# MLP down projections in seven quadrant products, their sums carried through PSUM by ScalarE, with a feature-major output

## The chip, the core and the metric

The kernel runs on one core of one Trainium2 chip. A core has TensorE (PE) for matrix products, which reads SBUF and writes PSUM; VectorE (DVE) and ScalarE (ACT) for element-wise work on both memories; GpSimd (POOL), which is little used here; and SyncE (SP), which issues nearly all DMA loads. Each engine runs its own instructions in order and waits on semaphores for the others. The metric is device time of one execution in microseconds (us), the median of three runs.

## What is computed

A trunk of two layers over 512 tokens with 1024 features: a latent-attention mixer (MLA), then a gated linear attention mixer (GLA). Each is followed by a squared-ReLU MLP with 4096 hidden features. Only the MLP and the last norm change.

```python
def sq_relu_mlp(xn, w_up, w_down):
    hid = jnp.square(jax.nn.relu(xn @ w_up))
    return hid @ w_down
...
for i in range(DEPTH):                       # 2: MLA, GLA
    x = x + mixer(rms_norm(x, norm_mix[i]))
    x = x + sq_relu_mlp(rms_norm(x, norm_mlp[i]), w_up[i], w_down[i])
return rms_norm(x, final_norm)
```

## The kernel before

**Layout.** The residual stream lies in SBUF feature-major: `xT[j]` holds features 128j to 128j+127 on the partitions and 512 tokens along the free dimension. A weight tile of 128 by 128 is the stationary operand, and up to 512 tokens stream past it. All products are made in float32 accuracy from two rounded halves: a value is split into `hi` (a rounding ScalarE copy, line 76) and `lo` (a VectorE subtraction, line 79), and `mm3` (lines 81 to 86) issues three matmuls, hi by hi, hi by lo, lo by hi. A `piece` (line 109) is such a split of 1024 weight values per partition, in three rotating buffers `wh` and `wl`. So every piece costs one ScalarE and one VectorE instruction, and a piece feeds 24 matmuls.

**Order.** The kernel is written as straight-line Python. A planner puts each engine's instructions in order: by the order of the source where it can, and otherwise an instruction that is ready earlier goes first. Tiles with the same tag share a fixed number of buffers; an instruction that needs a buffer waits until its last reader is done. SP's loads wait in the same way, one behind the other.

**Up projection.** 4096 hidden features are handled in 8 blocks of 512 (`FB`). The first block, `up(0)` (line 715), is a plain product: 96 matmuls of 512 tokens. Blocks 1 to 7 are made by `up_fast` (line 825) in seven products of quadrants instead of eight, after Strassen and Winograd: the weights are halved by input features and by output features, the activations by features and by tokens (`first`, `second`: tokens 0 to 255 and 256 to 511). The sums of activation quadrants, T1 to T4, are made once per layer by `quadrants` (line 806); the sums of weight quadrants are VectorE instructions on 1024 values per partition, once per block (lines 855, 856, 864, 865). Each product has 24 matmuls of 256 tokens. Its result is added to others by VectorE (`add`, line 840); `finish` (line 843) applies ReLU, the norm's factor `nrm.rstd` and the square, and splits the result for the down projection.

**Down projection.** `down` (line 736) is a plain product: for each block of 512 hidden features 8 output tiles of 12 matmuls over 512 tokens. VectorE adds each result from PSUM into `xT` (line 750). For the last block of the last layer `down_final` (line 756) makes tokens 0 to 255 feature-major and tokens 256 to 511 row-major, so that most of the last norm runs while PE still works. The class `Final` (line 1311) does that norm and writes two outputs.

**Around it.** `out_proj` (line 690) makes the mixers' output projection in four steps of two feature tiles, adds them to `xT` and calls `nxt.add`, which scales, splits and squares a tile for the next norm. `Norm.finish` (line 216) makes the mean with a matmul (line 218) and `rsqrt` with two ScalarE and three VectorE instructions. After the first MLP comes `gla` (line 895), whose first products use the norm's tiles in order. PSUM has eight banks of 512 float32 per partition, in three tags (`bank`, line 62).

Of the kernel before, what the change touches and what calls it, by code (L numbers as in the profile page):

```python
# [25 lines left out]
TH = S // 2  # L26
MH = 8
# [21 lines left out]
def trunk_kernel(ctx: ExitStack, tc: tile.TileContext, t_in: dict, out: bass.AP, out_row: bass.AP):  # L49
# [5 lines left out]
    ps = ctx.enter_context(tc.tile_pool(name="ps", bufs=1, space=bass.MemoryType.PSUM))  # L55
    count = [0]

# [4 lines left out]
    def bank(tag):  # L62
        return ps.tile([P, 512], F32, tag=f"ps_{tag}", bufs={"a": 2, "b": 3, "c": 3}[tag], name=uname("ps"))

    def tmp(shape=(P, 512), dt=F32):
        return sb.tile(list(shape), dt, tag="tmp", bufs=6, name=uname("tmp"))

    def slot(tag, shape=(P, 512)):
        return sb.tile(list(shape), F32R, tag=f"set_{tag}", bufs={"A": 16, "B": 16}[tag], name=uname("set"))
# [11 lines left out]
    def mm3(psum, w, x, start, stop):  # L81
        wh, wl = w
        xh, xl = x
        PE.matmul(psum, wh, xh, start=start, stop=False)  # L84
        PE.matmul(psum, wh, xl, start=False, stop=False)  # L85
        PE.matmul(psum, wl, xh, start=False, stop=stop)  # L86
# [17 lines left out]
    def load(src, a, n):  # L104
        raw = sb.tile([P, a, n], F32, tag="wraw", bufs=2, name=uname("wraw"))
        SP.dma_start(raw, src)
        return raw
# [78 lines left out]
    class Norm:  # L186
# [7 lines left out]
        def square(self, src):  # L194
            if self.seen == 0:
                self.acc = sb.tile([P, S], F32, tag="acc", bufs=2, name=uname("acc"))
# [19 lines left out]
        def finish(self):  # L216
            m = bank("c")
            PE.matmul(m, self.inv, self.acc, start=True, stop=True)  # L218
            r = sb.tile([P, S], F32, tag="rstd", bufs=2, name=uname("rstd"))
            rsqrt(r, m, S)  # L220
            self.rstd = r
            return r

# [103 lines left out]
    def mla(layer, nrm, first, pools):  # L327
# [70 lines left out]
        rows = sb.tile([3 * RB, S], F32, tag="rstd", bufs=2, name=uname("rstd"))  # L398
# [3 lines left out]
        raw = sb.tile([P, 2, MH, VD], F32, tag="wraw", bufs=2, name="wraw_v")  # L402
# [12 lines left out]
        for t in range(NT):  # L415
# [18 lines left out]
            if t == 1:  # L434
                wide = bank("c")
                PE.matmul(wide, ones128[0:1], rows[0:1], start=True, stop=True)
                r_kv = sb.tile([P, S], F32, tag="rstd", bufs=2, name=uname("rstd"))
# [21 lines left out]
        raw = sb.tile([P, 3, MH, ROPE], F32, tag="wraw", bufs=2, name="wraw_qr")  # L459
# [18 lines left out]
        def project(h, tag="a"):  # L478
            if h % 4 == 0:
                raw = sb.tile([P, 3, 4, NOPE], F32, tag="wraw", bufs=2, name=uname("wraw_qn"))  # L480
# [3 lines left out]
                raw = sb.tile([P, 2, 4, NOPE], F32, tag="wraw", bufs=2, name=uname("wraw_kn"))  # L484
# [191 lines left out]

    def out_start(w2d, X, n):
        raw = col_chunk(w2d, 0, 256)
        w = [piece(raw[:, :, j * P : (j + 1) * P], ND, P) for j in range(2)]
# [10 lines left out]
    def out_proj(w2d, X, nxt, begun=None):  # L690
        for c in range(4):
# [3 lines left out]
            else:  # L695
                raw = col_chunk(w2d, c * 256, 256)
                w = [piece(raw[:, :, j * P : (j + 1) * P], ND, P) for j in range(2)]
# [3 lines left out]
            for j in range(2):  # L701
                m = 2 * c + j
                DVE.tensor_tensor(xT[m], ps_[j], xT[m], ALU.add)
                nxt.add(m, xT[m])


    def mlp(layer, nrm, tag, nxt, final=False):
        w_up, w_dn = t_in["mlp_w_up"][layer], t_in["mlp_w_down"][layer]
        X = nrm.out
        NB = FF // FB  # L710

        es = ExitStack()
        fast = es.enter_context(tc.tile_pool(name=f"fast{layer}", bufs=1, reuse_waits="tile"))

        def up(b):
            hid = []
            for c in range(2):
                raw = col_chunk(w_up, b * FB + c * 256, 256)
                w = [piece(raw[:, :, j * P : (j + 1) * P], ND, P) for j in range(2)]
                ps_ = [bank("ac"[c]), bank("ac"[c])]  # L720
                if b == 0 and c == 0:
                    a_pair(ps_, w, nrm)
                else:
                    for j in range(2):
                        a_type(ps_[j], w[j], X)
# [30 lines left out]
        def down_final(b, hid):  # L756
# [16 lines left out]
            for t in (2, 3):  # L773
                tk = slice(t * P, (t + 1) * P)
                ps_ = [bank("ac"[t % 2]) for _ in range(2)]
                for c in range(2):
# [4 lines left out]
                    if t == 2:  # L781
# [7 lines left out]
                        if c == 0:  # L789
                            nxt.finish()  # L790
# [639 lines left out]
```

## Time and profile before

| | |
|---|---|
| median of 3 runs | 1108.24 us (1108.23 to 1108.47) |
| span of the profiled execution, first to last instruction | 1105.7 us |
| instructions | 15687, of which 6310 matmuls |
| first MLP, as PE sees it | 191.0 to 527.5 us |
| second MLP | 758.2 us to the end |
| HBM traffic | 98.35 MB read, 91 GB/s over the span |

The profile is of one execution, and its times are measured from its first instruction. A matmul row gives the time until its result stands, so the rows of a stream overlap; what a stream costs is the distance from start to start. Busy time of an engine is the time in which at least one of its instructions ran. A window row gives, for one stretch of time, that busy time for every engine, with the number of instructions in brackets.

### The profile page before, as it was taken

What the parts mean: (1) busy time and instruction counts of PE and PEld (TensorE: products, weight loads), DVE (VectorE), ACT (ScalarE), POOL (GpSimd) and SP (SyncE); (2) the same over time, 40 slices, a digit from 0 to 9 for tenths busy, and PEclk for the clock granted to TensorE, in tenths of its full rate; (3) what the DMA queues carried; (4) which work ended last, traced back from release to release, by engine and by line L of the source; (5) the groups of instructions that cost most, each with busy time, mean ns of one, the idle gap of its engine ahead of it and who ended that gap; (6) DMA issues with size and microseconds to landing.
All of it is one profiled execution on the core that took longest, in us unless ns stands there. A gap on an engine that the chain in (4) does not pass through costs nothing.

```text
span 1105.7 us, 15687 instructions
## 1 busy us (share of the span) xinstructions
PE 1095.0 (99%) x6310; PEld 961.9 (87%) x6310; DVE 827.1 (75%) x1314; ACT 528.6 (48%) x868; POOL 41.7 (4%) x78
## 2 busy tenths in 40 slices
PE   8999999999999999999999999999999999999997
PEld 7788888899899899898788888888989989989986
DVE  6789867988778788776565654669878878878865
ACT  6576654644344344344335735645534434434434
POOL 6410002000000000000000000000000000000000
PEclk9999999999999999999999999999999999999999
DMA  7312123232332332322322222222333233233212
GB/s 220 78 48 77 39 76 114 69 123 77 114 115 77 114 115 77 114 76 77 87 75 77 77 76 77 77 82 79 107 114 115 76 114 115 76 115 115 96 39 76
DMA packets 86024, 101.45 MB, mean 92 GB/s; under 512 B 7376, under 2 KB 63968, under 8 KB 85952
## 3 DMA queue, kind: packets, MB, share of 16 engines
q1 hardware_dynamic: 83936, 99.23, 28.3%
q10 hardware_dynamic: 1952, 1.21, 0.4%
q8 instruction: 49, 0.80, 0.3%
q0 software_dynamic: 64, 0.02, 0.1%
q14 instruction: 23, 0.19, 0.1%
HBM read 98.35 MB, written 2.10 MB: 91 GB/s over the span
## 4 chain that ended last, share of the span: by engine, by line
PE 98%; DMA 1%; ACT 0%; issue 0%; DVE 0%; SPq 0%; DVEq 0%
PE ps L84 30%; PE ps L86 30%; PE ps L85 30%; PE ps L101 2%; PE ps L1106 2%; DMA wraw_ckv<-in_mla_w_in_dram 1%; PE ps L593 0%; PE ps L1143 0%; PE ps L594 0%; PE ps L591 0%; PE ps L592 0%; PE ps L590 0%; PE ps L1112 0%; PE ps L1092 0%; PE ps L218 0%
## 5 line engine op out<-in xcount | busy, mean ns | idle before, releaser
L84 PE MATMUL ps<-set,wh 128*128 128x512 f32 (+1 forms) x1112 | 399.0, 359 | 1.4 <-ACT set L208 1.4
L85 PE MATMUL ps<-set,wh 128*128 128x512 f32 (+1 forms) x1112 | 397.6, 358 | 0.9 <-DVE set L209 0.8
L86 PE MATMUL ps<-set,wl 128*128 128x512 f32 (+1 forms) x1112 | 397.4, 357 | 0.0
L76 ACT ACTIVATE wh<-wraw 128x1024 fp32r<-128x1024 f32 x139 | 146.9, 1060 | 295.1 <-PE ps L85 230.7
L84 PEld LDWEIGHTS ps<-set,wh 128*128 128x128 f32 x1112 | 210.0, 189 | 32.7 <-ACT set L208 2.0
L85 PEld LDWEIGHTS ps<-set,wh 128*128 128x128 f32 x1112 | 210.1, 189 | 32.3 <-DVE set L209 1.6
L86 PEld LDWEIGHTS ps<-set,wl 128*128 128x128 f32 x1112 | 210.1, 189 | 30.3
L79 DVE TENSOR_TENSOR wl<-wraw,wh 128x1024 fp32r<-128x1024 f32 x139 | 169.9, 1223 | 38.2 <-ACT wh L76 38.1
L750 DVE TENSOR_TENSOR xT<-ps,xT 128x512 f32<-128x512 f32 x120 | 82.5, 688 | 60.4 <-PE ps L86 60.4
L840 DVE TENSOR_TENSOR tmp<-ps,tmp 128x512 f32<-128x512 f32 x98 | 67.4, 687 | 25.1 <-PE ps L86 25.1
L76 ACT ACTIVATE wh<-comb 128x1024 fp32r<-128x1024 f32 x42 | 44.4, 1056 | 82.8 <-PE ps L85 82.8
L84 PE MATMUL ps<-wh,set 128*128 128x512 f32 x144 | 59.5, 413 | 0.0
L79 DVE TENSOR_TENSOR set<-tmp,set 128x256 fp32r<-128x256 f32 (+1 forms) x128 | 53.4, 439 | 8.0 <-ACT set L76 7.7
L86 PE MATMUL ps<-wh,set 128*128 128x512 f32 x144 | 56.4, 391 | 0.0
L85 PE MATMUL ps<-wl,set 128*128 128x512 f32 x144 | 56.3, 391 | 0.0
L79 DVE TENSOR_TENSOR wl<-comb,wh 128x1024 fp32r<-128x1024 f32 x42 | 51.3, 1222 | 6.6 <-ACT wh L76 6.6
L846 ACT ACTIVATE tmp<-tmp 128x512 f32<-128x512 f32 x56 | 35.2, 628 | 35.7 <-DVE tmp L845 35.7
L76 ACT ACTIVATE set<-tmp 128x256 fp32r<-128x256 f32 (+1 forms) x128 | 48.8, 425 | 2.0
L76 ACT ACTIVATE wh<-raw 128x1024 fp32r<-128x1024 f32 x28 | 29.4, 1052 | 23.0 <-PE ps L85 23.0
L845 DVE SCALAR_TENSOR_TENSOR tmp<-tmp,rstd 128x512 f32<-128x512 f32 x56 | 38.6, 689 | 0.9
L79 DVE TENSOR_TENSOR wl<-raw,wh 128x1024 fp32r<-128x1024 f32 x28 | 34.1, 1218 | 0.0
L86 PEld LDWEIGHTS ps<-wh,set 128*128 128x128 f32 x144 | 27.0, 188 | 5.8
(372 smaller groups left out, 1877.8 us busy)
## 6 DMA issues: line engine op xcount, KB each, us to landing
wraw<-in_mlp_w_up_dram SPq DMA_DIRECT2D x32, 1024.0 KB, 5.5
wraw<-in_mlp_w_down_dram SPq DMA_DIRECT2D x18, 1024.0 KB, 5.1
raw<-in_mlp_w_down_dram SPq DMA_DIRECT2D x14, 1024.0 KB, 5.1
wraw<-in_gla_w_in_dram SPq DMA_DIRECT2D x12, 1024.0 KB, 5.1
wraw<-in_mla_w_o_dram SPq DMA_DIRECT2D x4, 1024.0 KB, 5.1
wraw<-in_gla_w_o_dram SPq DMA_DIRECT2D x4, 1024.0 KB, 5.1
xT<-in_x_dram SPq DMA_DIRECT2D x6, 256.0 KB, 7.2
wraw_qn<-in_mla_w_uq_dram SPq DMA_DIRECT2D x6, 256.0 KB, 3.5
```

The costliest lines, as they stand in the source:

```text
L76: order(ACT.activation(hi, src, AF.Copy))
L79: lo_eng.tensor_tensor(lo, src, f(hi), ALU.subtract)
L84: PE.matmul(psum, wh, xh, start=start, stop=False)
L85: PE.matmul(psum, wh, xl, start=False, stop=False)
L86: PE.matmul(psum, wl, xh, start=False, stop=stop)
L101: PE.transpose(psum, src, ident[: src.shape[0], : src.shape[0]])
L750: DVE.tensor_tensor(xT[m], p, xT[m], ALU.add)
L840: DVE.tensor_tensor(dst, p, t, ALU.add)
L845: DVE.scalar_tensor_tensor(c3, c3, 0.0, nrm.rstd[:, tk].unsqueeze(1).to_broadcast([P, 2, TH]), ALU.max, ALU.mult)
L846: ACT.activation(c, c, AF.Square)
L1106: PE.matmul(p[:, t * 64 : (t + 1) * 64].rearrange("p (n c) -> p n c", c=m), k[:, sl], later, start=True, stop=True)
```

## The change

**Up projection.** All eight blocks are now made in seven products; the plain `up(0)` is gone. The activation sums T1 to T4 are made inside `out_proj`, one pair of feature tiles after each of its steps (`QuadNorm.pair`); to that end `out_proj` takes tiles c and c+4 together, and their weights come in two loads of 512 KB. In a block, some products are now added in PSUM: a result is copied by ScalarE from one bank into another (`seed`) and the next product accumulates on it. The hidden values are no longer split here; they are kept as float32 in quadrant tiles `q`.

**Down projection.** Two blocks of hidden features (1024) are taken together, and the 1024 by 1024 weights, halved both ways, are multiplied with the hidden quadrants in seven products of 48 matmuls of 256 tokens. There are four such groups per layer. Sums of weight quadrants (2048 values per partition) and of hidden quadrants (1024 values) are made by VectorE in each group; each of the seven hidden operands is split once. The seven running sums `acc` lie in SBUF, four of them in `xT` itself. Before a product, ScalarE copies its running sum into two PSUM banks, PE accumulates on it, and ScalarE copies it back. In the first group VectorE adds four of the results instead, and in the last group VectorE combines the seven sums (`u2`, `u3`).

**Order.** Up products and down products are interleaved in the source: the down group of blocks 0 and 1 among the up products of blocks 2 and 3, and so on. The first two up blocks and the last down group stand alone.

**Memory.** Pools are opened and closed by stage: the mixers' staging pool and slots make room for the MLP's `up` and `down` pools and come back afterwards. PSUM in the MLP is one bank `seed`, three banks `u` and two double banks `d`. `acc` and `rstd` have one buffer instead of two. The masks of `gla` are made inside `gla`.

**Output.** The last norm is made by token halves, feature-major, in `Final.quarter`, and there is one output.

```diff
-        def down(b, hid):
...
-                        p = bank("b")
-                        a_type(p, w, hid, cols=slice(j * P, (j + 1) * P))
-                        DVE.tensor_tensor(xT[m], p, xT[m], ALU.add)
...
+            def product(n, a, t, evac=None):
+                x = operand(t)
+                p = mp.tile([P, 4 * TH], F32, tag="d", bufs=2, name=uname("ps"))
+                p4 = p.rearrange("p (m t) -> p m t", m=4)
+                begin = s == 0
+                if not begin:
+                    ACT.activation(p4, acc[n], AF.Copy)
...
+                    for h in range(2):
+                        w = piece(a[:, 2 * h : 2 * h + 2], 2, 512)
+                        matmuls(p, w, 2 * h, (2 * h, 2 * h + 1), range(4), x, begin, True, lambda m: m)
+                if evac is not None:
+                    evac(p4)
+                elif begin and n in (2, 3, 4, 5):
+                    DVE.tensor_tensor(acc[n], p4, acc[n], ALU.add)
+                else:
+                    ACT.activation(acc[n], p4, AF.Copy)
...
+            def p6():
+                DVE.tensor_tensor(v["S"], v["S"], v["11"], ALU.subtract)
+                DVE.tensor_tensor(b11, b22, b11, ALU.subtract)
+                def u2(p4):
+                    DVE.tensor_tensor(acc[6], p4, acc[1], ALU.add)
+                    DVE.tensor_tensor(acc[2], acc[2], acc[1], ALU.add)
+                    DVE.tensor_tensor(acc[5], acc[5], acc[6], ALU.add)
+                    DVE.tensor_tensor(acc[3], acc[3], acc[5], ALU.add)
+                product(6, v["S"], b11, u2 if last else None)
...
+            return [p1, p5, p6, p7, p3, p2, p4_] if last and final else [p1, p5, p6, p7, p2, p3, p4_]
...
-        hid = up(0)
-        quadrants()
         for b in range(NB):
...
+            for i, step in enumerate(up_block(b)):
+                step()
+                if b == 0 and i == 0:
+                    begin()
+                if i % 2 or (b % 2 and i == 6):
+                    if downs:
+                        downs.pop(0)()
+            if b % 2:
+                downs += down_block(b // 2)
+        closed("up")
+        nxt.open()
+        for step in downs:
+            step()
```

An up block in the new kernel, with its products in the order of the source (in block 0 the second and third change places); `x1`, `x5` and `b2` are PSUM banks, and `False` means that the product accumulates on what stands there:

```python
def s1():
...
    product(v["x1"], a, "11", True)
...
    ACT.activation(v["b2"], v["x1"], AF.Copy)
def s5():
...
    DVE.tensor_tensor(s, v["a21"], v["a22"], ALU.add)
...
    product(v["x5"], s, "T1", True)
...
def s7():
    DVE.tensor_tensor(v["a21"], v["a11"], v["a21"], ALU.subtract)
    product(v["b2"], v["a21"], "T3", False)
...
    DVE.tensor_tensor(c, pairs(v["b2"]), pairs(v["p5"]), ALU.add)
    finish(c, 1, second)
def s4():
    product(v["b2"], v["a22"], "T4", False)
    finish(pairs(v["b2"]), 1, first)
return [s1, s2, s5, s6, s3, s7, s4] if b == 0 else [s1, s5, s2, s6, s3, s7, s4]
```

571 lines of the change are left out of this document (309 added, 262 removed).

## The prediction

> **What bounds the kernel now.** I read the page's busy times first, then its slices and chain, then starts in the timeline of PE.
>
> ```profile
> span 1105.7 us, 15687 instructions
> PE 1095.0 (99%) x6310; PEld 961.9 (87%) x6310; DVE 827.1 (75%) x1314; ACT 528.6 (48%) x868; POOL 41.7 (4%) x78
> ...
> PE   8999999999999999999999999999999999999997
> ...
> PEclk9999999999999999999999999999999999999999
> ...
> PE 98%; DMA 1%; ACT 0%; issue 0%; DVE 0%; SPq 0%; DVEq 0%
> ```
>
> PE works without a gap, at full granted clock, and is 98% of the chain of waits. So time is matmuls times their distance from start to start. Four rows of PE's timeline give it: 73 matmuls of 256 tokens between the first two rows, 82 of 512 between the last two.
>
> ```profile
> 224.82 0.28 PE L86 MATMUL ps<-T3h,wl 128*128 128x256 f32 x1
> ...
> 233.35 0.28 PE L86 MATMUL ps<-set,wl 128*128 128x256 f32 x1
> 400.61 0.40 PE L85 MATMUL ps<-set,wh 128*128 128x512 f32 x1
> ...
> 418.99 0.39 PE L85 MATMUL ps<-set,wh 128*128 128x512 f32 x1
> ```
>
> 256 tokens: 8.53 / 72 = 0.1185 us. 512 tokens: 18.38 / 81 = 0.2269 us. Two narrow ones cost 0.237, 4% more than one wide one for the same work, which takes a third of the one eighth that seven products instead of eight save. The windows of both MLPs, of the stretch after the first's start, and of one up block with the down block behind it:
>
> ```profile
> 191.00:527.50 336.50, 336.50 (x2044) 302.15 (x2043) 265.39 (x342) 148.41 (x206) 1.06 (x2) 1.00 0.30 97
> 758.20:1105.70 347.50, 340.81 (x2118) 307.79 (x2117) 267.43 (x368) 151.54 (x228) 0.00 (x0) 1.00 0.29 95
> 198.00:213.00 15.00, 15.00 (x66) 12.16 (x65) 13.69 (x17) 8.67 (x12) 0.00 (x0) 1.00 0.22 70
> 261.80:281.70 19.90, 19.90 (x144) 18.79 (x143) 17.67 (x27) 11.82 (x19) 0.00 (x0) 1.00 0.33 106
> 281.70:303.40 21.70, 21.70 (x123) 19.05 (x122) 14.94 (x16) 5.32 (x6) 0.00 (x0) 1.00 0.30 97
> ```
>
> Columns: length, then busy time of PE, weight loads, VectorE, ScalarE, GpSimd, the clock, DMA. VectorE is at 79% of the first MLP (265.4 of 336.5) and at 91% in 198 to 213, yet PE never waited. A first MLP counts 1176 narrow and 864 wide matmuls: 139.4 + 196.0 = 335.4, and 336.5 was measured, so its seams cost 1.1.
>
> **The change on PE.** A layer now has 8 x 168 up and 4 x 336 down matmuls, all narrow: 2688 x 0.1185 = 318.5, and with the same 1.1 for seams 319.6. That is 16.9 less than the 336.5 of now, per layer, if PE stays fed. The Trainium skill, page "TensorE: Matmul & The Clock Gate", section "Back-to-back issue gap", gives N/2.4 + 2.5 ns for a warm matmul alone, 109 and 216 ns here. By that a layer would save 21 and the end would be some 9 us earlier than mine; the trace has 118.5 and 226.9 ns, and I use the trace.
>
> **What must feed it.** Durations from the groups by line and form:
>
> ```profile
> L79 DVE TENSOR_TENSOR wl<-wraw,wh 128x1024 fp32r<-128x1024 f32 x139 | 169.9, 1223 | 38.2 <-ACT wh L76 38.1
> L750 DVE TENSOR_TENSOR xT<-ps,xT 128x512 f32<-128x512 f32 x120 | 82.5, 688 | 60.4 <-PE ps L86 60.4
> L209 DVE SCALAR_TENSOR_TENSOR set<-xT,gains,set 128x512 fp32r<-128x512 f32 x32 | 23.8, 756 | 3.6 <-ACT set L208 3.6
> L816 DVE SCALAR_TENSOR_TENSOR comb<-xT,gains,comb 128x256 f32<-128x256 f32 x8 | 3.9, 486 | 0.3
> L1346 DVE TENSOR_TENSOR o<-o,rstd 128x256 f32<-128x256 f32 x8 | 2.8, 419 | 0.0
> L76 ACT ACTIVATE wh<-wraw 128x1024 fp32r<-128x1024 f32 x139 | 146.9, 1060 | 295.1 <-PE ps L85 230.7 <-PE ps L86 41.4 <-issue 21.2
> L846 ACT ACTIVATE tmp<-tmp 128x512 f32<-128x512 f32 x56 | 35.2, 628 | 35.7 <-DVE tmp L845 35.7
> L853 ACT ACTIVATE tmp<-ps 128x512 f32<-128x512 f32 x14 | 8.1, 581 | 0.0
> ```
>
> L1346: eight of 0.419 took 2.8, so VectorE's instructions overlap by 0.07: 1.15 for 1024 values, 0.62 for 512, 0.35 for 256. No row has 2048 values: at least 2 x 1.15 less one fixed part, 2.1, at most 2 x 1.22 = 2.44; with 0.53 per further 512 (1.22 less 0.69) it is 2.29, overlapped 2.22, which I take.
>
> VectorE, up block: 7 splits and 4 weight sums of 1.15, 2 adds and 4 `finish` of 0.62: 16.4, beside 19.9 of PE (now about 22.3, with 7 adds and 8 small splits). Down group: 7 operand and 14 weight splits and 4 hidden sums of 1.15, 4 weight sums of 2.22: 37.6 beside 39.8. A pair of up blocks with a group: 70.4 of 79.6, 88%. The first group adds 4 x 1.15 (94%), the last 7 x 1.15: 45.7 beside 39.8, above PE.
>
> ScalarE, up block: 7 x 1.06, 3 copies of 0.58, 4 squares of 0.63: 11.7. Group: 21 splits of 1.06, 7 copies back of 1.0 (0.58 and 0.43 more), 7 copies into PSUM. No row has ScalarE writing PSUM: at least 1.0, as its read of PSUM, at most 2.1, twice the split's 1.06, to which it is nearest in form and which I take. Together 60 of 79.6; at 2.1 it is 67.5, still below PE. The copies hide: two double banks leave a whole product, 5.7, for one copy back and one seed.
>
> So in the middle PE stays the bound, and I charge 1.0 per layer for waits there. Three places lack cover.
>
> **Start, per layer.** `up(0)` was cover of 21.8 us for making T1 to T4; now the third product needs T1. After the last `out_proj` matmul VectorE adds (0.69), splits and sums the last tile (0.75, 0.69) and makes four sums (1.9); ScalarE and VectorE split T (1.06, 1.22), and a waiting weight piece takes 1.22: 7.5, less 0.5 of overlap, 7.0. The buffer for the weight sum is freed only then: sum, two splits, 3.5. That is 10.5.
>
> ```profile
> 197.82 0.86 PE ps L218 x2
> ```
>
> PE has two products of 2.84, the norm's matmul above and one of 0.23 to do: 6.8. It waits 3.7; then 0.7 for the next weight sum (3.5 against 2.84), twice 0.9 in the two blocks without down products, where `s4` writes the bank that VectorE still reads (0.69 and hand-offs), and 1.0 for the three rsqrt instructions that compete. Sum 7.2, taken as 7. Bounds: 3 if the planner puts T first and frees a buffer early, 12 if the rsqrt goes ahead.
>
> **Last group, per layer.** VectorE can be ahead by one product's splits and the next sums (6.8), no more: three `wl`, two operand buffers. By the start of the sixth product (28.4 into the group) it needs 33.1 of work: the second to fifth products' 3.45 + 6.8 + 6.8 + 3.45 (three splits each, in two of them both sums), `u2` 4.6, two of the three of `u3` 2.3, the sixth's 5.7; for `u2` and `u3` must be done before the sums are seeded. PE waits 4 (0 if they slip into gaps, 9 without a lead). In layer 1 `Final` adds squares, folds and scalings on both engines: 6 (0 to 14).
>
> **Into `gla`, once.**
>
> ```profile
> wraw<-in_gla_w_in_dram SPq DMA_DIRECT2D x12, 1024.0 KB, 5.1
> ```
>
> Its first weights (1 MB, 5.1 us to landing) now go where the hidden quadrants lay. Those are read for the last time before the last product (5.7), so a load and a split (2.3) nearly hide: 1.5 (0 to 8).
>
> **End.** The last matmuls and instructions now:
>
> ```profile
> 1098.12 0.91 PE ps L793 x8
> ...
> 1090.61 0.46 ACT L95 ACTIVATE tmp<-ps,eps_t 128x256 f32<-128x256 f32 x1
> ...
> 1092.47 0.42 DVE L184 SCALAR_TENSOR_TENSOR rstd<-tmp,tmp 128x256 f32<-128x256 f32 x1
> ...
> 1101.09 0.55 DVE L1375 TENSOR_SCALAR fin_row<-fin_row,sm 128x640 f32<-128x640 f32 x1
> ```
>
> Now 6.7 from PE's end (1099.03) to the span's. After the change: a square 0.6, two mean matmuls 0.9, the rsqrt 2.3 (1090.61 to 1092.89), four multiplications 2.5, hand-offs 0.3, and as now 4.1 from the last VectorE instruction to the end: 10.7 (9 to 14).
>
> **At nothing:** `pair` inside `out_proj` (VectorE 8.6 of 10.9 us per step; uncovered 2.3 per step); one 1 MB load more per group and loads of 512 KB (DMA 30% busy; SP waits in order, and a late one costs its 5.1); masks on idle GpSimd; one buffer for `acc` and `rstd`, whose readers are done by then.
>
> **Sum.** First MLP: 319.6 + 7 + 1 + 4 + 1.5 = 333.1 against 336.5: -3.4. Second: 319.6 + 7 + 1 + 6 + 10.7 = 344.3 against 347.5: -3.2. Together -6.6. The median is 2.5 above the profiled span, which I leave: 1108.2 - 6.6 = **1101.6 us**. So of 34 us that PE saves (twice 16.9), 27 are given back in waits.
>
> **Rivals.**
> *Lumps on VectorE (slower).* Products 5, 6 and 7 put a weight sum, a hidden sum and an operand split on VectorE in one go: 2.29 + 1.22 + 1.22 = 4.7. Pieces are at most two ahead, 5.7, of which a split takes 2.3, so 3.4 are left: PE waits 1.3 wherever the planner issues the lump ahead of a due piece. 24 such products, all paying: 31 us, 1133; half of them: **1117**. It decides from 5 of 24 on. For it: 88 to 94% load and strict order. Against: 91% in 198 to 213 with no wait, and fewer instructions that wait on PE in the middle than now. 0.33.
> *Run-ahead hides more (faster).* The planner spreads the sums, and the waits at the starts, in the last groups and into `gla` (14 + 10 + 1.5) halve: 12.7 less, **1089**; all gone, 1076. For it: an up block now holds more VectorE work (22.3) than PE time, with no wait. 0.19.
> *The clock falls.* PE has not idled here, so its clock (9 in all slices) was never tested. If after each start's wait it ran at half clock for one product, that is 2.84 twice: **1107**, no change. The Trainium skill, same page, section "Why this matters for your kernels", warns of idle gaps over about 3 us for this; no run here shows it yet. 0.12.
> *My forecast*, 1095 to 1106: 0.36.
>
> A measurement here can tell 0.2%, 2.2 us, from no change. Faster: 0.36 + 0.19 = 0.55. Same 0.12, slower 0.33. The range goes from 1083, where the starts and the last groups wait for almost nothing, to 1128, where most lumps pay; I leave out some 0.15.
>
> **What would show it.** Starts 0.1185 apart throughout; 2 x 2688 narrow MLP matmuls; idle time of PE at the two starts before the third up product, some 4 us in one piece, released by a `wl` or T split; VectorE above 95% in the last groups; the copies into PSUM near 1.06; PEclk below 9 after a start if the clock rival holds. I am wrong if PE idles in the middle, product by product (lumps), or if SP's loads release it.

## The result and the profile after

The changed kernel is slower: 1120.91 us (median of 4, 1119.84 to 1122.13) against 1108.36 beside it; ratio 1.0110, 95% interval 1.0095 to 1.0124. Forecast was 1101.6, 6.6 us less, with 1083 to 1128 as range: the time lies inside the range, but it moved the other way. In the experiments below, one execution each of e1 (1371.8 us), of e7 (2822.8) and of e9 (1505.7, the one that was profiled) lies far outside the others and is left out of all comparisons.

The page of the changed kernel, busy times, slices and the chain of waits:

```profile
span 1119.2 us, 18319 instructions
PE 1067.7 (95%) x7540; PEld 988.0 (88%) x7540; DVE 919.2 (82%) x1195; ACT 679.5 (61%) x965; POOL 47.0 (4%) x78
...
PE   8999999899999999987799999998999999999976
...
PEclk9999999999999999999799999999999999999999
...
PE 22%; DVE 3%; issue 1%; ACT 1%; DVEq 0%; ACTq 0%
```

PE's busy time fell from 1095.0 to 1067.7, as the change meant. But PE's row has a hole just before the middle, and PEclk falls there too. The chain covers only 27% of the span here, the part from about 815 us on, so it says nothing of the first MLP. The place to look is the end of the first MLP. The span cut at the matmuls that open and close its stages, in the windows of the changed kernel (length, then PE, weight loads, VectorE, ScalarE, GpSimd, clock, DMA):

```profile
192.50:248.02 55.52, 49.07 (x390) 46.88 (x389) 53.13 (x57) 31.04 (x39) 0.00 (x0) 0.97 0.41 134
248.02:471.40 223.38, 222.25 (x1922) 221.65 (x1921) 202.25 (x182) 150.88 (x170) 0.00 (x0) 1.00 0.35 114
471.40:526.15 54.75, 49.24 (x387) 48.30 (x385) 49.51 (x42) 37.25 (x44) 10.22 (x13) 0.94 0.29 97
526.15:541.14 14.99, 4.11 (x13) 2.35 (x11) 10.78 (x17) 10.07 (x16) 2.50 (x5) 0.67 0.11 18
541.14:774.43 233.29, 233.22 (x1196) 196.19 (x1196) 137.86 (x242) 109.22 (x206) 0.00 (x0) 0.99 0.24 73
774.43:829.26 54.83, 47.98 (x389) 45.92 (x388) 53.13 (x57) 30.94 (x39) 0.00 (x0) 1.00 0.41 135
829.26:1053.62 224.36, 224.19 (x1921) 223.78 (x1920) 202.19 (x182) 150.74 (x170) 0.00 (x0) 1.00 0.35 113
1053.62:1106.75 53.13, 46.56 (x388) 45.67 (x387) 52.09 (x48) 38.65 (x49) 0.00 (x0) 1.00 0.19 61
1106.75:1119.20 12.45, 1.82 (x9) 1.14 (x7) 5.40 (x11) 3.43 (x8) 0.00 (x0) 0.83 0.51 168
```

Start is the stretch from the last `out_proj` matmul to the first hidden matmul, 384 narrow ones; the middle has 1920; the last stretch (last up product to last down matmul) has 384. The forecast, put on the same cuts with 0.1185 a matmul, adds up to 1099.1, which is 1105.7 - 6.6:

| stage | forecast | measured | off |
|---|---|---|---|
| head | 191.0 | 192.5 | +1.5 |
| start, layer 0 | 45.5 + 1.1 + 7 = 53.6 | 55.5 | +1.9 |
| middle, layer 0 | 227.5 + 1 = 228.5 | 223.4 | -5.1 |
| last stretch, layer 0 | 45.5 + 4 = 49.5 | 54.8 | +5.3 |
| seam into `gla` | 1.5 | 15.0 | **+13.5** |
| `gla` and its `out_proj` | 230.7 | 233.3 | +2.6 |
| start, layer 1 | 53.6 | 54.8 | +1.2 |
| middle, layer 1 | 228.5 | 224.4 | -4.1 |
| last stretch, layer 1 | 45.5 + 6 = 51.5 | 53.1 | +1.6 |
| end | 10.7 | 12.4 | +1.7 |

These differences make +20.1: 1119.2 instead of 1099.1. Two thirds of it is one seam, the stretch between the last down matmul of the first MLP and the first product of `gla`. Without these 13.5 us the span would be 1105.7, that of the kernel before, so the change would still have gained nothing. What PE waits for there, by the timeline of PE:

```profile
526.15 0.28 PE L110 MATMUL ps<-hh,wl 128*128 128x256 f32 x1
533.45 2.07 PE L242 MATMUL ps<-acc,inv 128*128 128x512 f32 x2 [7.02 <-DVE acc L225]
539.38 1.83 PE L1101 MATMUL ps<-one_t,rstd 1*128 1x1 f32 x8 [3.86 <-DVE rstd L208]
541.14 0.80 PE L108 MATMUL ps<-set,wh 128*128 128x512 f32 x1
```

The norm's matmul L242 stands ahead of every `gla` product in PE's order and waits 7.0 us for the last sum of squares; then PE waits 3.9 us more for the rsqrt. Were the weights late? The DMA issues of 515 to 526 us, then the timelines of ScalarE and VectorE:

```profile
wraw<-in_gla_w_in_dram SPq DMA_DIRECT2D x2, 1024.0 KB, 6.6
```
```profile
531.45 0.62 ACT L224 ACTIVATE mt<-xT 128x512 f32<-128x512 f32 x1
535.56 0.69 ACT L119 ACTIVATE tmp<-ps,eps_t 128x512 f32<-128x512 f32 x1 [3.50 <-PE ps L242]
...
536.81 1.04 ACT L100 ACTIVATE wh<-wraw 128x1024 fp32r<-128x1024 f32 x1
```
```profile
538.54 0.69 DVE L208 SCALAR_TENSOR_TENSOR rstd<-tmp,tmp 128x512 f32<-128x512 f32 x1
539.15 2.35 DVE L103 TENSOR_TENSOR wl<-wraw,wh 128x1024 fp32r<-128x1024 f32 x2
```

Both loads were issued by 517 and took 6.6 us (median), so they landed before PE's last down matmul at 526. ScalarE sat idle for 3.5 us at 532 with the weights in memory, because the rsqrt stands ahead of the split in its order. So it looks like an order that the engines follow, not a load.

### The profile page after: what moved, and what is told of

Same layout as the page of the kernel before. It is cut to its first block, busy times and chain, and to the rows that moved or that the text cites. A ratio compares the mean times of both kernels' runs of the same rounds, so it can differ in the third digit from the quotient of the medians.

```text
span 1119.2 us, 18319 instructions
## 1 busy us (share of the span) xinstructions
PE 1067.7 (95%) x7540; PEld 988.0 (88%) x7540; DVE 919.2 (82%) x1195; ACT 679.5 (61%) x965; POOL 47.0 (4%) x78
## 5 line engine op out<-in xcount | busy, mean ns | idle before, releaser
L100 ACT ACTIVATE wh<-raw 128x1024 fp32r<-128x1024 f32 x224 | 236.3, 1059 | 174.0 <-PE ps L109 123.5
L103 DVE TENSOR_TENSOR wl<-raw,wh 128x1024 fp32r<-128x1024 f32 x224 | 270.0, 1218 | 31.9 <-ACT wh L100 31.3
L110 PE MATMUL ps<-hh,wl 128*128 128x256 f32 x896 | 252.9, 282 | 9.6 <-DVE wl L103 9.5
L108 PE MATMUL ps<-hh,wh 128*128 128x256 f32 x896 | 252.6, 282 | 2.9 <-ACT ps L903 2.9
L109 PE MATMUL ps<-hl,wh 128*128 128x256 f32 x896 | 252.3, 282 | 0.0
L110 PEld LDWEIGHTS ps<-hh,wl 128*128 128x128 f32 x896 | 170.2, 190 | 11.0 <-DVE wl L103 11.0
L108 PEld LDWEIGHTS ps<-hh,wh 128*128 128x128 f32 x896 | 170.2, 190 | 3.5 <-ACT ps L903 3.3
L109 PEld LDWEIGHTS ps<-hl,wh 128*128 128x128 f32 x896 | 170.1, 190 | 0.2
L109 PE MATMUL ps<-set,wh 128*128 128x512 f32 x232 | 92.4, 398 | 1.2 <-DVE set L233 1.2
L108 PE MATMUL ps<-set,wh 128*128 128x512 f32 x232 | 93.0, 402 | 0.5 <-ACT set L232 0.4
L109 PEld LDWEIGHTS ps<-set,wh 128*128 128x128 f32 x232 | 44.0, 190 | 12.0 <-DVE set L233 2.3
L108 PEld LDWEIGHTS ps<-set,wh 128*128 128x128 f32 x232 | 44.0, 190 | 10.9 <-ACT set L232 1.4
```

What stands on the lines that cost most here:

```text
L100: order(ACT.activation(hi, src, AF.Copy))
L103: lo_eng.tensor_tensor(lo, src, f(hi), ALU.subtract)
L108: PE.matmul(psum, wh, xh, start=start, stop=False, **kw)
L109: PE.matmul(psum, wh, xl, start=False, stop=False, **kw)
L110: PE.matmul(psum, wl, xh, start=False, stop=stop, **kw)
```

## The experiments

e1 to e4 were made from the changed kernel; e5, e6 and e8 to e12 stand on top of e2; e7 on the kernel before. Times are medians, with the ratio to the kernel before, measured beside each run, and its 95% interval. A cut in code is marked by three dots.

### e1: the norm's matmul keeps its place behind five tiles' products

```diff
-        def finish(self):
+        def finish(self, order=lambda i: i):
...
-            PE.matmul(m, self.inv, self.acc, start=True, stop=True)
+            order(PE.matmul(m, self.inv, self.acc, start=True, stop=True))
...
             if k == 5:
-                nrm.finish()
+                nrm.finish(tc.keep_in_program_order)
```

> The norm's matmul ahead of gla keeps its program place, behind the products of gla's first five feature tiles; nothing else is changed. Theory 'order': the 13 us in which PE stands at the seam (526.2 to 541.1 but for 2.2) come from the order of the engines: norm adds, then norm matmul, then rsqrt, then weight splits. Then the weight splits come 3 to 4 us earlier, the rsqrt hides behind products, and the run is 5 to 8 us shorter than the changed kernel's 1120.9: 1113 to 1116. The 7 us before the last add stay. Theory 'load' (the one in the prediction): the weights come late; the order changes nothing: 1120 to 1122.

### e2: gla's first weights early

```diff
         def open(self):
             opened("wide", "right")
+            self.raw = opened("early", "right").tile([P, ND, 256], F32, tag="first", name="first_raw")
+            SP.dma_start(self.raw, t_in["gla_w_in"][0][:, :256].rearrange("(k p) n -> p k n", p=P))
...
         def quarter(self, n, src, dst):
             if n == 5:
                 return
+            if n == 4:
+                self.w0 = [piece(self.raw[:, :, j * P : (j + 1) * P], ND, P) for j in range(2)]
...
         def proj_qk(c):
-            raw = col_chunk(w_in, c * 256, 256)
-            w = [piece(raw[:, :, j * P : (j + 1) * P], ND, P) for j in range(2)]
+            if c == 0:
+                w = nrm.w0
+            else:
+                raw = col_chunk(w_in, c * 256, 256)
+                w = [piece(raw[:, :, j * P : (j + 1) * P], ND, P) for j in range(2)]
```

> gla's first weights are loaded into memory on the side that the up blocks left, and their two pieces are split ahead of the last four norm tiles instead of behind them. Both theories expect a gain here, of different size from the first run's: 'order' expects the first gla product within 2 us of the last down product (the first four norm tiles are long ready), so 11 to 15 us less than 1120.9: 1106 to 1110, of which the first run already has 5 to 8. 'Load' expects all 11 to 15 here and nothing in the first run. If only the clock counted (half speed after the wait, some 3 us here), both would give 2 to 3.

Seam and `gla` in the windows of e1, then of e2, and the first weight splits of `gla` in e1's timeline of ScalarE (536.81 in the changed kernel):

```profile
526.09:533.00 6.91, 0.28 (x4) 0.07 (x2) 6.33 (x11) 6.91 (x13) 2.51 (x5) 0.67 0.00 0
533.00:769.66 236.66, 236.14 (x1205) 197.48 (x1206) 142.35 (x248) 112.44 (x210) 0.00 (x0) 0.99 0.24 73
```
```profile
526.36:526.48 0.12, 0.12 (x4) 0.12 (x2) 0.12 (x1) 0.12 (x2) 0.00 (x0) 1.00 0.00 0
526.48:762.70 236.22, 234.28 (x1207) 195.69 (x1206) 147.93 (x258) 119.04 (x222) 3.15 (x5) 1.00 0.23 69
```
```profile
531.90 2.94 ACT L100 ACTIVATE wh<-wraw 128x1024 fp32r<-128x1024 f32 x3
```

Order alone takes the seam from 15.0 to 6.9 us, with the same loads at the same place. That cannot be if the load were late. Early pieces take it to 0.1. `gla` itself grows by 3.4 and 2.9, since the norm's matmul and waits for late norm tiles now lie in it; seam and `gla` together go from 248.3 to 243.6 (-4.7) and 236.3 (-11.9). In time e2 is 1112.13 (ratio 1.0029, 1.0015 to 1.0043), 8.8 less than the changed kernel, short of the 11 to 15 expected; e1 is 1118.19 (1.0085, 1.0065 to 1.0105), only 2.7 less, short of its 5 to 8: in the profiled execution of e1 its start and last stretch in layer 1 were 4.5 longer, at a lower clock, and its last stretch in layer 0 was 3.2 shorter, at a higher one (below). The seam itself behaves as "order" has it; the load theory, that of the prediction, falls.

### e3: the start of each layer

```diff
-                self.any = hi
+                if j == KH:
+                    self.any = hi
...
+        def lead(self):
+            w_up = t_in["mlp_w_up"][self.g0 // ND]
+            self.a11 = pool_of("up").tile([P, KH, 256], F32, tag="raw", bufs=5, name=uname("raw"))
+            SP.dma_start(self.a11, w_up[:512, :256].rearrange("(k p) n -> p k n", p=P))
+            self.w11 = piece(self.a11, KH, 256)
...
+            if c == 3:
+                nxt.lead()
...
-                w = piece(a, KH, 256)
+                w = nrm.w11 if a is nrm.a11 else piece(a, KH, 256)
...
-                s = v["s"] = up.tile([P, KH, 256], F32, tag="raw", bufs=5, name=uname("raw"))
+                s = v["s"] = up.tile([P, KH, 256], F32, tag="raw", bufs=5, name=uname("raw")) if b else nrm.last
```

`lead` is called ahead of the last two tiles' adds; `nrm.last` is the last pair's tile.

> The first up weights of each layer are loaded and split ahead of the last two tiles' adds, the sum for T1 goes into the last pair's own buffer, and the matmul that opens the bank reads the first trailing tile instead of the last. Theory 'order': the two waits of 1.46 and 1.47 us at each start go (PE begins s1 at once), and with them the spell at half clock in layer 0 (1.7 us): 2 to 3 per layer, together 4 to 7 less: 1114 to 1117. Rival 'VectorE chain': adds, split, sums and splits of T take 7 us whatever stands before them, and PE waits as long in front of the third product: less than 1.5 in all, 1119.5 to 1121.

Measured: 1121.26 (1.0122, 1.0099 to 1.0144). Start windows of e3, layers 0 and 1, then two waits at the first start in the timeline of PE, of the changed kernel and of e3:

```profile
193.21:248.68 55.47, 50.84 (x389) 48.99 (x388) 53.77 (x57) 31.23 (x39) 0.00 (x0) 0.94 0.41 134
775.81:830.38 54.57, 49.99 (x389) 48.00 (x388) 53.60 (x57) 31.25 (x39) 0.00 (x0) 0.97 0.42 136
```
```profile
194.41 0.50 PE L984 MATMUL ps<-x7h 128*128 128x512 f32 x1 [1.31 <-ACT x7h L262]
196.11 0.38 PE L110 MATMUL ps<-x0h,wl 128*128 128x256 f32 x1 [1.20 <-DVE wl L103]
```
```profile
203.17 0.39 PE L108 MATMUL ps<-T0h,wh 128*128 128x256 f32 x1 [1.28 <-ACT wh L100]
205.55 0.58 PE L110 MATMUL ps<-T0h,wl 128*128 128x256 f32 x1 [1.88 <-DVE wl L103]
```

The two early waits are gone, but PE now waits longer in front of and inside the third product. The start is 55.5 and 54.6, as before it (55.5, 54.8), so in length the rival was right. PE's idle time did fall, from 6.5 and 6.9 us to 4.6 and 4.6, but the clock is lower in both starts (0.94 and 0.97 against 0.97 and 1.00). Beside starts of other runs at the same clock, shown under e6, those of e3 are 0.7 to 1.3 us shorter, so order gave about that, not 2 to 3. VectorE is busy for 53.8 of 55.5 us, which speaks for the chain on VectorE as what sets the rest.

### e4: weight sums in halves

```diff
+            def two(o, a, b, op):
+                for h in range(2):
+                    c = slice(2 * h, 2 * h + 2)
+                    DVE.tensor_tensor(o[:, c], a[:, c], b[:, c], op)
...
-                DVE.tensor_tensor(v["S"], v["21"], v["S"], ALU.add)
+                two(v["S"], v["21"], v["S"], ALU.add)
```

The same for the other three weight sums.

> Each VectorE instruction over 2048 weight sums of the down groups becomes two over 1024 values. Theory 'lump': PE's waits of 2.0 us in the last groups (three in each layer) are a 2.28 us sum in front of a due weight split; in halves the split waits 1.2 less: 2 to 5 us less in all, 1116 to 1119, and no spell at half clock in the last group of layer 0. Rival 'VectorE full': the last group has more VectorE work than PE time in any order, so the waits keep their sum: within 1 us of 1120.9, or 1 to 2 above for 28 more fixed parts of 0.07 each.

Measured: 1131.57 (1.0211, 1.0156 to 1.0266), 10.7 more than the changed kernel, which neither theory had. The last stretches got no shorter (54.8 as before; 56.1 against 53.1, at a clock of 0.94 against 1.00). New waits came in the middle (230.2 us against 223.4), of this kind in VectorE's timeline:

```profile
351.05 1.23 DVE L889 TENSOR_TENSOR raw<-raw,raw 128x1024 f32<-128x1024 f32 x1 [2.20 <-DMA raw<-in_mlp_w_down_dram]
```

VectorE waited for a half sum whose load had not landed, and PE waited 2.5 us for a split behind it (up to 354.66). Since the sums now meet their loads in another way, this run does not price a weight sum in front of a due split.

### e5: sums on GpSimd

```diff
+            side = POOL if last else DVE
...
-                DVE.tensor_tensor(b11, b12, b11, ALU.subtract)
+                side.tensor_tensor(b11, b12, b11, ALU.subtract)
```

The same for the three other hidden sums and for `acc[2] += acc[1]`.

> On top of the early gla weights: in the last group of each layer the four sums of hidden quadrants and one sum of accumulators, 1024 values each, run on GpSimd instead of VectorE. Theory 'VectorE full': products five, six and seven each ask VectorE for a 2.28 us weight sum, a 1.2 us hidden sum and three 1.22 us splits, 7.1 us against 5.7 of PE, so the waits of 2.0 us there are work that does not fit; with 1.15 less for each of the five sums they shrink from 4.0 (layer 0) and 5.1 (layer 1) to under 2 each, and with them go spells at half clock: 3 to 8 us less than the 1112.1 of the early weights. Rival 'order': the waits come from one weight sum ahead of one due split, and stay at 2.0 each: within 1.5 of 1112.1. If GpSimd takes over 4 us for a sum, its latency makes new waits on hh: slower than 1112.1.

Measured: 1123.88 (1.0149, 1.0122 to 1.0177), 11.8 more than e2. GpSimd and VectorE in e5's timeline at the same time:

```profile
477.50 3.28 POOL L948 TENSOR_TENSOR q<-q,q 128x1024 f32<-128x1024 f32 x1
```
```profile
475.61 6.25 DVE L103 TENSOR_TENSOR wl<-raw,wh 128x1024 fp32r<-128x1024 f32 x2
...
492.00 4.36 DVE L935 TENSOR_TENSOR raw<-raw,raw 128x2048 f32<-128x2048 f32 x1
```

A sum takes GpSimd 2.4 to 4.4 us, and VectorE is held up beside it: two splits take 6.25 instead of 2.35, a weight sum 4.36 instead of 2.28. These two rows alone lose 6.0 us, and the five sums that left VectorE are worth 5 x 1.15 = 5.8. So nothing was taken off VectorE. The Trainium skill, page "SBUF — State Buffer", section "SBUF: two separate sides", says that the two engines share a port pair under an exclusive lock; these rows agree with it.

### e6: PE kept busy at the starts

```diff
+FILL = 12
+FILL5 = 7
...
-                self.any = hi
+                if j == KH:
+                    self.any = hi
...
+                if b == 0:
+                    for _ in range(FILL5):
+                        PE.matmul(v["x5"], nrm.any[:, :P], nrm.any, start=True, stop=True)
...
-        PE.matmul(t, nrm.any[:, :P], nrm.any, start=True, stop=True)
+        for _ in range(FILL):
+            PE.matmul(t, nrm.any[:, :P], nrm.any, start=True, stop=True)
```

> On top of the early gla weights: PE does work that nothing reads while it waits at the start of each layer. The matmul that opens the bank reads the first trailing tile and runs 12 times (2.7 us, about the wait there), and 7 more (1.6 us) stand ahead of the product that waits for T1. Theory 'clock': an idle stretch of 1.5 to 3 us costs more than itself, for the 4.1 us after it run at half clock (196 to 200 and 766 to 770 with the early weights); with PE kept busy no slice there shows under 1.0, and the run is 3 to 4 us shorter than 1112.1 though no work is saved. Rival 'idle only': the clock follows something else; the spells stay, and the time stays at 1112.1 or rises by what the extra matmuls overshoot, 0 to 2.

Measured: 1114.81 (1.0060, 1.0045 to 1.0075), 2.7 more than e2, above what both theories had. The first start of e6 (the second is as long, 56.47, also at 1.00), then those of e2 (the clock is third from the right):

```profile
193.54:250.02 56.48, 52.98 (x407) 49.73 (x406) 54.46 (x58) 30.95 (x39) 0.00 (x0) 1.00 0.40 131
```
```profile
193.13:248.90 55.77, 49.74 (x390) 47.68 (x389) 53.49 (x57) 31.03 (x39) 0.00 (x0) 0.97 0.42 133
762.70:818.55 55.85, 49.83 (x389) 47.77 (x388) 53.49 (x57) 31.03 (x39) 0.00 (x0) 0.97 0.40 132
```

With PE kept busy neither start has a spell at half clock (a spell is a stretch in which the granted clock is 0.5). One profile alone would not show that idle time brings the spells, since starts with these waits come without one too (e1's first, below). But the mean granted clock of all four executions of e6 is 0.991, against 0.987 for the eight of e2, and two spells of 3.4 us less at half clock would make 0.003 of it. So the clock part of the theory is supported, and its price is not: 18 extra matmuls (18 x 0.227 = 4.1 us) overshoot the waits, and the start grows by 0.6 to 0.7.

What comes before a spell, in the changed kernel: a wait in the last stretch of layer 0 and the clock behind it (0.84 in 491 to 495 and 0.74 in 495 to 499, so 3.4 us at 0.5), then the longest wait in the last stretch of layer 1, which stays at a clock of 1.00:

```profile
492.84 0.39 PE L110 MATMUL ps<-hh,wl 128*128 128x256 f32 x1 [1.81 <-DVE wl L103]
```
```profile
493.00:497.00 4.00, 4.00 (x22) 4.00 (x23) 4.00 (x3) 2.17 (x3) 0.00 (x0) 0.59 0.23 88
```
```profile
1089.32 0.39 PE L108 MATMUL ps<-hh,wh 128*128 128x256 f32 x1 [2.89 <-ACT ps L903]
```

The price of a spell is better read where the same instructions ran with and without one. e1's first start, its last stretch in layer 0 (beside 54.75 at 0.94 above), and its second start:

```profile
194.87:249.47 54.60, 47.99 (x389) 45.83 (x388) 52.90 (x57) 30.95 (x39) 0.00 (x0) 1.00 0.41 136
...
474.55:526.09 51.54, 46.12 (x387) 45.21 (x385) 49.12 (x42) 37.18 (x44) 17.35 (x13) 1.00 0.31 103
...
769.66:825.87 56.21, 50.79 (x389) 48.97 (x388) 53.65 (x57) 31.38 (x39) 0.00 (x0) 0.94 0.41 132
```

Starts take 54.6 and 54.8 us at 1.00, 55.5 to 55.8 at 0.97 and 56.2 at 0.94: one spell costs a start 0.7 to 1.3 us, two in the last stretch 3.2. The same kernel meets more or fewer of them: eight executions of e2 lie between 1108.84 and 1114.79, at mean clocks of 0.983 to 0.991, while those of the kernel before lie within 2.2 us.

### e8: no weight sums in the last groups

```diff
+            def total(o, a, b, op):
+                if not last:
+                    DVE.tensor_tensor(o, a, b, op)
```

All four weight sums go through `total`, so the last groups leave out part of the computation.

> On top of the early gla weights: the four weight sums of 2048 values in the last down group of each layer are left out, and its products take the weights as loaded, so part of the computation is missing. PE's work is the same. Theory 'VectorE full': from 478 to 518 VectorE had no idle time, so 4 x 2.28 = 9.1 us less there lets PE run on: the stretch from the last up product to the last down matmul (384 matmuls, 44.7 us of PE at 0.1165; 53.7 and 53.5 with the early weights) falls to 45 to 47 in both layers, and the run to 1095 to 1099. Rival 'latency': PE waits for a chain of hand-offs (copy into PSUM, operand split, accumulator sums), which stays: 51 to 53 us a stretch, 1107 to 1111.

Measured: 1098.75 (0.9903, 0.9885 to 0.9922), within "VectorE full". VectorE in 478 to 518 us of e2, then the last stretches of e8, layers 0 and 1:

```profile
478.00:518.00 40.00, 35.69 (x269) 34.59 (x268) 39.71 (x32) 26.97 (x28) 9.24 (x12) 0.91 0.23 73
```
```profile
475.76:522.48 46.72, 45.07 (x387) 44.87 (x385) 41.58 (x38) 36.86 (x44) 9.86 (x13) 1.00 0.40 136
...
1037.21:1086.45 49.24, 47.29 (x388) 46.89 (x387) 44.10 (x44) 38.34 (x49) 0.00 (x0) 0.97 0.20 66
```

VectorE was busy for 39.7 of 40 us. With 9.1 us less of work per layer the stretches fall from 53.7 and 53.5 to 46.7 and 49.2 (45 to 47 was expected in both), near PE's own 44.7. So the waits in the last groups come from VectorE's weight sums, not from hand-offs; in layer 1 4.5 us remain above 44.7, beside `Final`'s work. Part of the 7.0 us in layer 0 is the clock, 0.94 in e2 and 1.00 here. A rival is not parted from "VectorE full": that one long sum stands in front of a due split, since e8 takes out sum and load together. That VectorE had 0.3 us idle in 40 speaks for the load.

### e7, e9 and e10: addresses

One point of the table ran the other way: the middles are 9.2 us faster than forecast. Narrow matmuls are 223.38 / 1920 = 0.1163 apart there, and 0.1185 before; in `out_proj` wide ones went from 0.2267 to 0.2334. The matmuls have the same form; where the tiles lie differs, and so do the banks and what other engines do beside them. e7, e9 and e10 change only the place of tiles. e7 puts 32 unused bytes ahead of all tiles of the kernel before; e9 puts 1248 behind the pieces and 64 at the right end; e10 puts the weight pieces first. Their edits, in this order:

```diff
+    const.tile([P, 8], F32, name="pad")
     ident = const.tile([P, P], F32, name="ident")
```
```diff
+    ctx.enter_context(tc.tile_pool(name="gap", bufs=1)).tile([P, 312], F32, name="gap")
...
+    ctx.enter_context(tc.tile_pool(name="rpad", bufs=1, side="right")).tile([P, 16], F32, name="pad")
```
```diff
+    sb = ctx.enter_context(tc.tile_pool(name="sb", bufs=1))
     const = ctx.enter_context(tc.tile_pool(name="const", bufs=1))
-    sb = ctx.enter_context(tc.tile_pool(name="sb", bufs=1))
```

> The kernel before with an unused 32 bytes per partition ahead of all its tiles, so that every tile on the left side of memory stands 32 bytes further; no instruction changes. Theory 'address': the distance between matmuls depends on where in memory the operands start (512 tokens: 0.2267 us before, with the activations at 32 beyond a multiple of 128 bytes; 0.2333 after, at 64; 256 tokens: 0.1185 before and 0.1153 after). Then this run has about 0.233 for 512 tokens and is 15 to 25 us slower than 1108.4. Rival: the distance follows what the other engines do at the same time, or the layout of the banks: 0.2267 and 1108.4 as before, within 1 us.

> On top of the early gla weights: 1248 unused bytes behind the weight pieces and 64 at the outer end of the right side, so that weight pieces, activations, T and hidden operands all start at the same offset modulo 2048 bytes (1952), as weight pieces and activations did in the kernel before (1440); no instruction changes. Theory 'offset': the distance between matmuls depends on the offset of the moving operand against the weights'. Then 512 tokens go from 0.2333 back to 0.2270 in out_proj and gla, and the hidden operands' 256 tokens from 0.1172 to about 0.1150: 5 to 9 us less than 1112.1. Rival: the distance does not depend on addresses; 0.2333 stays, within 1.5 of 1112.1.

> On top of the early gla weights: the weight pieces stand ahead of the residual in memory instead of behind it (they start at 128 modulo 2048 instead of 1952; activations stay at 704 and 2016); no instruction changes. Theory 'offset': distances between matmuls change in some stage by over 0.001 us (which way isn't known). Rival 'no address': every stage as with the early weights, 0.2333 in out_proj, 0.114 to 0.116 for x and T, 0.1172 for hidden operands.

e7: 1108.41 (1.0002, 0.9993 to 1.0012), no change where 15 to 25 more was expected: shifting weights and activations together does nothing. e9: 1122.21 (1.0118, 1.0099 to 1.0138), 10.1 slower than e2 where 5 to 9 faster was expected. Its profile can't be read for distances; why it is slow stays open. e10, one execution: 1116.53. The last matmuls of `out_proj` in the timelines of PE, of the changed kernel (69 matmuls), then of e10 (70):

```profile
176.61 0.39 PE L108 MATMUL ps<-set,wh 128*128 128x512 f32 x1
...
192.48 0.40 PE L110 MATMUL ps<-set,wl 128*128 128x512 f32 x1
```
```profile
176.70 0.39 PE L109 MATMUL ps<-set,wh 128*128 128x512 f32 x1
...
192.50 0.39 PE L109 MATMUL ps<-set,wh 128*128 128x512 f32 x1
```

15.87 / 68 = 0.2334, and 15.80 / 69 = 0.2290. In e10 pieces and these activations start at the same offset modulo 64 bytes, in the changed kernel 32 apart. T (the activation sums), which e10 parts from the pieces by 32, went to 0.1200 (71 steps from 357.06 to 365.58), against 0.1133 (49 steps from 353.74 to 359.29) and 0.1177 (71 steps from 936.09 to 944.45) in the changed kernel. So T also varies by 0.004 at one and the same place, and e10 lies above that. e9, with all of them at the same offset modulo 64, should have been fast by such a rule, and was not.

### e11 and e12: plain last groups

The last group of each layer without sums of quadrants: each output quadrant is two plain products, added in one PSUM tile; 48 matmuls more. The running sums are combined one group earlier, and the first four norm tiles are added one product earlier.

```diff
-            last = s == NB // 2 - 1
+            last = s == NB // 2 - 2
...
+            if s == NB // 2 - 1:
+                return [lambda n=n: plain(n) for n in (5, 3, 2, 4)]
```

e12 adds 32 bytes behind the pieces.

> On top of the early gla weights: the last down group of each layer is computed in eight plain quadrant products (four sums of two) instead of seven, with no sums of weights or hidden quadrants; the sums carried between products are combined at the end of the group before. PE gets 48 matmuls more per layer (5.6 us), VectorE in the last group some 25 us of work instead of 45. Theory 'VectorE full': the stretch from the last up product to the last down matmul is now PE's own 432 matmuls, 50.3 us, plus 1, against 53.7 and 53.5: 2 to 3 us less per layer, 1105 to 1109 in all. It goes wrong if the combining adds (5 x 1.15 us a layer) overfill VectorE in the group before (88% of its time is taken): then waits of 2 us appear there and the run is at 1111 to 1114.

> The run with plain last groups, and 32 unused bytes behind the weight pieces, so that activations on the left side and hidden operands start at the same offset modulo 64 bytes (32) as the weight pieces; no instruction changes. Theory 'offset modulo 64' (from the look with the weight pieces moved: out_proj went from 0.2334 to 0.2292 where pieces and activations came to the same offset, x and T from 0.115 to 0.120 where they parted): out_proj 0.2334 to 0.229, hidden operands 0.1172 to 0.115 or less, x and T as before: 3 to 6 us less than the run without the 32 bytes. Rival: chance, distances as without the 32 bytes and the time within 1.5.

Last stretches of e11, now of 432 matmuls:

```profile
473.57:525.81 52.24, 50.93 (x434) 50.53 (x433) 30.81 (x30) 34.52 (x41) 1.55 (x4) 1.00 0.42 142
...
1040.12:1091.41 51.29, 51.10 (x436) 50.86 (x435) 31.50 (x33) 33.84 (x44) 0.00 (x0) 1.00 0.31 104
```

52.2 and 51.3 (51.3 expected), with VectorE at 31 us instead of 50 and 52, and no spell at half clock. e11 takes 1108.26 us (ratio 1.0004, 0.9994 to 1.0015): the loss of the change is repaired, and the kernel before is not beaten. e12 takes 1108.31 (1.0000, 0.9992 to 1.0009), no faster than e11. In it `out_proj` is at 0.2290, as expected:

```profile
176.80 0.39 PE L111 MATMUL ps<-set,wl 128*128 128x512 f32 x1
...
192.37 0.39 PE L110 MATMUL ps<-set,wh 128*128 128x512 f32 x1
```

15.57 / 68 = 0.2290. Hidden operands stayed at 0.1177 (47 steps from 393.02 to 398.55), so the lower distance at the same offset modulo 64 is seen in `out_proj`, in two layouts, and not for all operands; what sets the narrow distance stays open.

## Why the prediction was wrong

- **"Into `gla`, once" failed**: 1.5 us, 8 at most, for a load that starts late. Measured 15.0. The load was in time. The sum has no term for the order there: the last down product ends with four tiles' adds, squares, norm matmul and rsqrt, and these stand ahead of the weight splits and products of `gla` on three engines. e1 and e2 show it: 8.1 of it goes by order alone (4.7 net of what `gla` gives back), all of it with early pieces (11.9 net). In the source `finish` stands behind the products of five tiles; the engines got another order.
- **The sign** would have failed without the seam too: the rest adds up to the span of the kernel before. The last stretches took 6.9 more than forecast, `gla`, the starts, the end and the head 8.9 more, and the middles 9.2 less, by a distance of matmuls that was not forecast. That gain is luck, and so is that 1120.9 lies near the 1117 of the rival of lumps, whose waits in the middle did not come.
- **Last group**: mechanism right (more VectorE work, 45.7, than PE time). PE stood idle for 5.5 us in layer 0 (54.75 less 49.24 busy) and 6.6 in layer 1 (53.13 less 46.56), against 4 and 6. What the sum lacked is the clock: above PE's own 44.7 the stretches took 10.1 and 8.4, and in layer 0 some 3 of it are two spells at half clock. I let VectorE start the stretch 6.8 us ahead, a head start that a middle at 90% may not have left it (argued, not tested). e8 agrees with the load, e11 removes it.
- **Start**: right in size. 7 was forecast, and PE stood idle for 6.5 and 6.9. It is right in place only in part: some 4 us in one piece before the third product was said, and no wait is over 1.7; 2.5 of it stand ahead of the third product, for the tile that opens the bank and a weight split (e3).
- **Middle**: right that nothing waits; the rival of lumps is wrong: the middles' windows have PE busy for 222.3 of 223.4 and 224.2 of 224.4 us, VectorE at 90 to 91%.
- **Clock**: the rival came true in size more than in place. It put 5.7 us on the clock; one spell at a start (0.7), two in the last stretch (3.2) and the end of one in `gla` (1.9) make some 5.8, an estimate. Half clock follows waits of 1.2 to 1.9 us at one start, twice in the last stretch of layer 0 and around the seam, and not each time (layer 1 of the changed kernel has such waits, one of 2.89, and a clock of 1.00). The Trainium skill, page "TensorE: Matmul & The Clock Gate", section "Why this matters for your kernels", puts the limit at idle gaps over about 3 us; here 1.8 was enough (the wait of 1.81 that ended at 492.84 in the changed kernel, with a clock of 0.59 in 493 to 497, and one of 1.83 that ended at 513.64, with 0.68 in 515 to 519).
- **Distance of matmuls**: 0.1185 taken over, 0.1163 and 0.1169 found in the middles, 9 us to the good; wide ones in `out_proj` 0.2334 instead of 0.2267, part of the +1.5 of the head and the +2.6 of `gla`. Another part of the latter is the clock, 0.52 from 541.14 to 545.03, some 1.9 us.
- **End**: 12.4 against 10.7, inside 9 to 14. The rsqrt (2.3), the multiplications (2.5) and the last 4.0 are as listed; not listed were two VectorE instructions of 0.42 between square and mean matmuls, which themselves took 1.5 and not 0.9.
- **Fixed costs**: a weight sum of 2048 values took 2.28, as estimated (2.29). A copy from ScalarE into PSUM took 1.02, the lower bound and not the 2.1 that I took; ScalarE was not the limit either way.

The second MLP came out as forecast, 344.5 against 344.3 (from its first matmul at 774.67), but by luck: a middle 4.1 us shorter made up for start, last stretch and end, 4.5 longer. The first took 348.4 (192.71 to 541.14) against 333.1, and 13.5 of these 15.3 us are its seam.

## What to carry to other kernels

When a change moves the last work of a stage, write out for each engine what then stands ahead of the next stage's first products, the norm chain above all; a load that lands in time is no cover if its split is queued behind that chain. An engine at 90% on average is full wherever a stretch lacks its usual partner work: sum its work by stretch, without credit for a head start that the average doesn't leave. And allow some 1 us more for a wait of 2 us on PE: in this case half clock followed some of them, at 0.7 to 1.6 us each.

## What the runs showed of the hardware that was not expected

- GpSimd's sums of two tiles in memory hold up VectorE's: 6.25 us for two splits that take 2.35, 4.36 for a sum that takes 2.28.
- Half clock for 3.4 us at a time after some of PE's waits of 1.2 to 1.9 us and not after others: 0.7 to 1.3 us each in the same start of the same code.
- The distance between equal matmuls changed when only the place of tiles changed: 0.2334 became 0.2290 for 512 tokens in `out_proj`, in two layouts (e10, e12), with weights and activations at the same offset modulo 64 bytes; shifting both together changed nothing (e7). The kernel before has 0.2267 there, at the same offset too, so this is not the whole rule.
